# RWKV-7 and convolution decoder layer on one core: `a` rows transposed whole, first splits queued behind the squares, LayerNorm sums queued behind the gate products

## The chip, the core and the metric

The kernel runs on one core of one Trainium2 chip. The metric is the device time of one execution in microseconds (us). A core has five engines that matter here, each working through its own instructions in a fixed order: TensorE (PE in the profile; its weight loads are PEld), VectorE (DVE), ScalarE (ACT), GpSimd (POOL) and SyncE (SP, which here only issues DMAs). They meet through semaphores: an instruction that waits holds back all that stands behind it on its engine.

## The reference

One layer (depth 1, width 1024) is applied to a prompt of 2048 tokens and to 8 single sample tokens with stored states. Cut to what matters:

```python
h = rms_norm(x, norm_pre_g)
proj = h @ w_in                      # r | k | v | z_rwkv | two loras | glu (2 x 512) | z_conv | two gates
ps = token_shift(proj[..., :N_SHIFT])
# branch A, 16 heads of 64: S_t = S_{t-1} diag(w_t) + (S_{t-1} a_t) b_t^T + v_t k_t^T ;  y_t = S_t r_t
o_r = (group_norm(y_w) + bonus) * silu(z_r)
# branch B
u = (u1 + b1) * sigmoid(u2 + b2)
c = causal_depthwise_conv(u, conv_w, width 31) + conv_b
cn = (c - mean(c)) * rsqrt(var(c) + LN_EPS) * ln_c_g + ln_c_b
o_c = silu(cn) * silu(z_c)
merged = sigmoid(g_r) * (o_r @ w_branch_r) + sigmoid(g_c) * (o_c @ w_branch_c)
y = x + rms_norm(merged @ w_out, norm_post_g)
```

The new shift row, wkv state and convolution state come out too. All is fp32.

## The kernel before

**Blocks, units, fills.** The prompt is cut into four blocks of 512 tokens, and channels lie on the 128 partitions. In each block a loop over eight units (`j`, two heads of 64 each) runs `unit_in` (the projections of r, k, v, z for a later unit), `unit_a` (L505, all that needs no state) and `unit_b` (L660, the chunked state recurrence). Between units `fill` adds the work of the tables `FILL0` (block 0, L301), `FILL1` (blocks 1 and 2) and `FILL2` (block 3), one string a unit: `u` is one tile of GLU and convolution, `n` the LayerNorm mean, `z` and `Z` the two pairs of convolution gates, and a digit one pair of branch gates. Then come the branch products (`merge`) and the output product (`stage_out`). The sample tokens ride along: their projections are 8 columns of the products of block 0, and their recurrence is spread over blocks 1 and 2.

**What sets the order.** A scheduler orders every engine's instructions when the kernel is built: it takes what its own estimates call ready, by priority and program order, and the result is fixed. `tc.high_priority` and `later` move the priority, and `tc.issue_after(i)` puts instructions of the same engine behind `i` (`behind` (L193) is the same for several). Buffers count: a tile of tag `tmp` has four buffers, `x` two, `w` five, `wraw` three (L70). PSUM has eight banks: three `pg`, two `pa`, one each of `pb`, `pc`, `py`.

**A product** (`gemm`, L311) is three passes (high, low, high parts) over eight row tiles, in `pg` banks. In the trace it reads `pg<-ht,w`, 512 columns wide, or 264 wide in block 0. Weights come from HBM once (`wraw`), are split into a high half by ACT and a low half by DVE, and the split pair is written back (`kept`) and read from there in later blocks (`load_split`, L144). `gemm_first` (L433) is the first such product: four column blocks by two weight halves.

**The first stage** (`stage_first`, L391) loads eight tiles of x, squares them on ACT, adds the squares on DVE, sums over channels on PE (`py<-tmp,avg_c`), and scales and splits the tiles into `ht`.

**`unit_a`.** `ar` holds the `a` rows and the `r` rows of 8 chunks of 64 tokens, as [128, chunk, 2, 64], and `bk` the b and k rows. 32 matmuls of 64 x 64 stationary (`pa<-ar,bk`) form the scores, DVE masks them into `W` (`sc<-pa,maskw`), ACT copies diagonal blocks to `gd`, and DVE solves 32 x 32 triangular systems (`gp`, `zr`, `gd`). PE needs that solve's result at `pb<-gd,sc`. Beside it, `a` is turned to tokens by 16 matmuls of 64 x 64 against the identity (`pa<-ident,ar`; in fp32 each leaves two records) and copied by one ACT instruction to `aw`; 16 more (`pa<-xv,sc`) give the other half of `aw`; and 8 whole transposes (`pa<-ident,bk`, L649) turn `bk`. Each writes one of the two `pa` banks in turn, so the first four `bk` transposes need the bank that the first `aw` copy empties.

**Convolution branch.** The 30 further taps of a tile are DVE instructions (`et<-u,cw,et`) given out by `pull`. `conv_norm` (L764) adds the four tiles, sums over channels on PE (`pg<-tmp,avg_c`, queued behind the last product by `done`) and subtracts the mean. `conv_scale` (L775) squares, sums on PE in the same way, and applies scale, shift and swish. `conv_gate` (L794) makes a pair of z products.

Of the kernel before, what the change touches and what calls it, by code (L numbers as in the profile page):

```python
# [25 lines left out]
def rwkv7_conformer_step(  # L26
# [274 lines left out]
    FILL0 = ("u1", "u2", "u3", "u5", "6n", "7", "0", "4zZ")  # L301
# [131 lines left out]
    def gemm_first(ht, cols):  # L433
# [3 lines left out]
        for h in range(2):  # L437
            for c0 in cols:
                ws[c0, h] = new([128, 2, 4, 128], "w", F32R)
                load_split(ws[c0, h], win(c0)[h], ("in", c0 // 128, h))  # L440
# [64 lines left out]
    def unit_a(b, j, tw, ins):  # L505
# [34 lines left out]
        ar = new([128, NC, 2, C], "ar")  # L540
        stt(ar[:, :, 0, :], c3(kkn), -1.0, ep[:, :, 0:C], ALU.mult, ALU.mult)
# [6 lines left out]
        mul(ar[:, :, 1, :], c3(R), ep[:, :, 1:C + 1])  # L548
# [111 lines left out]
    def unit_b(b, j, parts):  # L660
# [19 lines left out]
        for hf in range(2):  # L680
# [613 lines left out]
```

## Time and profile before

| | us |
|---|---|
| three runs | 2786.7, 2793.33, 2791.29 |
| their median | 2791.29 |
| the profiled execution | 2793.45 |
| its span in the profile | 2791.7 |

The profile is of one execution. Busy times overlap between engines. A row of the order in time gives start, length, engine, line, what is written from what, shapes and a count; idle time before it stands in brackets with what ended it. Most helper operations carry the helper's line (L94 for ACT, L100 and L106 for DVE, L112 for matmuls), so groups are told apart by tile names.

### The profile page before, as it was taken

To read this page: it belongs to the slowest core of one execution; us is meant where nothing else is said; L and a number is where in the kernel's file an instruction comes from. 1 tells how busy PE (TensorE), PEld (TensorE's weight loads), DVE (VectorE), ACT (ScalarE), POOL (GpSimd) and SP (SyncE) were. 2 spreads that over 40 slices of the span, in tenths; PEclk is the share of its full clock that TensorE was granted. 3 is DMA by queue.
4 is the path that set the end of the run, shared out by engine and by line. 5 is a ranking of instruction groups with operands and counts; after the bars stand their busy time and mean duration, and the time that the engine had idled before them with its cause. 6 is when DMAs were issued, how large, how long until landed. Compare 5 with 4: busy or idle time off the path is not lost.

```text
span 2791.7 us, 55435 instructions
## 1 busy us (share of the span) xinstructions
PE 2675.3 (96%) x22800; PEld 2133.7 (76%) x22800; DVE 1768.0 (63%) x3856; ACT 1388.4 (50%) x3039; POOL 16.2 (1%) x61
## 2 busy tenths in 40 slices
PE   6999999989999998999999999999999999999998
PEld 6888888878877776776887777677798777777787
DVE  5688887667876547556576646676376755664412
ACT  5666656672344555656113565755411356566511
POOL 0000000000000000000000000000000000000000
PEclk9999999999999899999999999999999999999999
DMA  6555654547974253344666324244466522332484
GB/s 215 184 166 179 196 179 167 188 136 257 312 248 135 86 146 114 109 147 130 212 235 214 129 94 156 100 134 150 154 215 215 193 95 100 96 114 92 132 280 166
DMA packets 149648, 458.50 MB, mean 164 GB/s; under 512 B 18897, under 2 KB 24258, under 8 KB 149387
## 3 DMA queue, kind: packets, MB, share of 16 engines
q1 hardware_dynamic: 143441, 433.36, 47.0%
q10 hardware_dynamic: 5954, 21.60, 1.9%
q8 instruction: 179, 2.93, 0.4%
q14 instruction: 74, 0.61, 0.1%
HBM read 346.21 MB, written 109.16 MB: 163 GB/s over the span
## 4 chain that ended last, share of the span: by engine, by line
PE 58%; DVE 20%; ACT 14%; DMA 4%; issue 2%; SPq 0%; POOL 0%; DVEq 0%; ACTq 0%; POOLq 0%
PE pg L112 41%; PE pa L112 7%; DVE gd L100 4%; PE pc L112 4%; PE py L112 4%; DVE zr L610 4%; PE pb L112 2%; ACT sc L94 2%; DVE et L106 2%; DVE raw L106 2%; DMA wraw<-in_w_in_dram 2%; ACT tmp L94 2%; ACT xv L94 2%; ACT zbuf L94 1%; ACT keep L94 1%
## 5 line engine op out<-in xcount | busy, mean ns | idle before, releaser
L112 PE MATMUL pg<-ht,w 128*128 128x512 f32 (+1 forms) x7200 | 1539.8, 365 | 18.2 <-DVE sconv L109 6.5
L112 PEld LDWEIGHTS pg<-ht,w 128*128 128x128 f32 x7200 | 1172.8, 190 | 264.6 <-issue 63.9
L106 DVE SCALAR_TENSOR_TENSOR et<-u,cw,et 128x512 f32<-128x512 f32 x480 | 359.5, 749 | 8.2
L94 ACT ACTIVATE raw<-pg,omm 128x512 f32<-128x512 f32 (+1 forms) x155 | 93.8, 605 | 194.0 <-PE pg L112 189.8
L94 ACT ACTIVATE tmp<-tmp 128x512 f32<-128x512 f32 (+1 forms) x305 | 185.5, 630 | 5.0 <-DVE tmp L106 2.5
L112 PE MATMUL pg<-orr,w 128*128 128x512 f32 (+2 forms) x960 | 184.7, 349 | 0.0
L112 PEld LDWEIGHTS pg<-orr,w 128*128 128x128 f32 x960 | 154.7, 188 | 25.0 <-DVE x L100 0.2
L94 ACT ACTIVATE w<-wraw 128x512 fp32r<-128x512 f32 x162 | 101.4, 629 | 119.5 <-PE pg L112 70.5
L106 DVE SCALAR_TENSOR_TENSOR raw<-pg,prm,raw 128x511 f32<-128x511 f32 (+1 forms) x185 | 103.8, 573 | 84.6 <-ACT raw L94 83.8
L100 DVE TENSOR_TENSOR gd<-zr,gp 128x144 f32<-128x144 f32 (+10 forms) x512 | 139.9, 273 | 15.2
L610 DVE TENSOR_REDUCE zr<-gd 128x16 f32<-128x32 f32 (+15 forms) x512 | 136.9, 267 | 13.9 <-DVE gd L100 0.2
L100 DVE TENSOR_TENSOR w<-wraw,w 128x512 fp32r<-128x512 f32 x162 | 110.6, 685 | 46.3 <-ACT w L94 45.2
L94 ACT ACTIVATE gd<-sc 32x128 f32<-32x128 f32 x256 | 78.6, 307 | 114.5 <-DVE sc L100 108.4
L528 DVE TENSOR_TENSOR_SCAN tmp<-scanm,tmp 128x512 f32<-128x512 bf16 x32 | 39.1, 1223 | 137.3 <-ACT tmp L94 137.3
L94 ACT ACTIVATE xs<-pc,dk 128x64 f32<-128x64 f32 x224 | 70.2, 313 | 106.5 <-PE pc L112 106.0
L100 DVE TENSOR_TENSOR x<-x,pg 128x512 f32<-128x512 f32 (+1 forms) x80 | 46.1, 578 | 101.5 <-PE pg L112 36.4
L112 PE MATMUL pa<-ar,bk 64*64 64x128 f32 x2048 | 101.3, 279 | 5.2 <-DVE bk L100 3.1
L112 PEld LDWEIGHTS pa<-ar,bk 64*64 64x64 f32 x2048 | 77.5, 132 | 37.1 <-DVE bk L100 15.1
L94 ACT ACTIVATE x<-pg 128x512 f32<-128x512 f32 (+1 forms) x80 | 40.9, 511 | 123.7 <-PE pg L112 119.9
L100 DVE TENSOR_TENSOR sc<-pa,maskw 128x512 f32<-128x512 f32 x128 | 82.5, 684 | 30.7 <-PE pa L112 30.3
L94 ACT ACTIVATE sc<-pa 64x256 f32<-64x256 f32 (+1 forms) x192 | 73.1, 381 | 47.0 <-PE pb L112 43.7
L100 DVE TENSOR_TENSOR keep<-pa,raw 128x512 f32<-128x512 f32 x32 | 22.1, 692 | 109.5 <-PE pa L112 109.5
(359 smaller groups left out, 3694.8 us busy)
## 6 DMA issues: line engine op xcount, KB each, us to landing
w<-kept_in SPq DMA_DIRECT2D x366, 512.0 KB, 3.4
kept_in<-w SPq DMA_DIRECT2D x122, 512.0 KB, 3.8
wraw<-in_w_in_dram SPq DMA_DIRECT2D x122, 256.0 KB, 3.2
w<-kept_br SPq DMA_DIRECT2D x48, 512.0 KB, 4.1
w<-kept_out SPq DMA_DIRECT2D x40, 512.0 KB, 4.5
gate<-x ACTq DMA_DIRECT2D x24, 512.0 KB, 4.7
x<-gate SPq DMA_DIRECT2D x48, 256.0 KB, 4.1
w<-kept_bc SPq DMA_DIRECT2D x24, 512.0 KB, 3.2
```

Of the source, the lines that this page charges most:

```text
L94: return nc.scalar.activation(out=out, in_=in_, func=func, scale=scale, bias=bias, **kw)
L100: return nc.vector.tensor_tensor(out=out, in0=a, in1=b, op=op)
L106: return nc.vector.scalar_tensor_tensor(out=out, in0=a, scalar=s, in1=b, op0=op0, op1=op1)
L112: return nc.tensor.matmul(out=out, lhsT=lhsT, rhs=rhs, start=start, stop=stop, **kw)
L528: nc.vector.tensor_tensor_scan(out=sw, data0=scanm.rearrange("p c t -> p (c t)"), data1=sw, initial=0.0, op0=ALU.mult, op1=ALU.add)
L610: nc.vector.tensor_reduce(out=zl[:, 0:n, t:t + 2], in_=pr[:, 0:n, :, 0:w], axis=AX.X, op=ALU.add)
```

## The change

- `ar` becomes [128, 2, chunk, 64], so all `a` rows lie side by side. Four whole 128 x 128 transposes take the place of the 16 matmuls, and four ACT copies of 64 partitions take the place of one of 128. The score matmuls now read their 128 columns as two pieces of 64.
- `conv_norm` is called at the end of the first gate pair and `conv_scale` at the end of the second, each with its sum behind that pair's products. The gate products are kept in `x` tiles instead of `tmp`, and multiplied in at the end of `conv_scale`.
- `FILL0` puts `z` and `Z` at units 5 and 6, and gates 0 and 4 last.
- The splits of the first weights are queued behind the last square on ACT and behind the last addition on DVE.
- In block 0 the copies of the 8 sample columns out of PSUM go from DVE (`vcp`) to ACT (`cp`).
- The copy of the old convolution states from HBM to HBM is issued in block 1 instead of at the start.
- In the last block the output tile is multiplied by `norm_post_g` straight out of PSUM, scaled and added to x in one DVE instruction a half, and written as two DMAs.

```diff
-    FILL0 = ("u1", "u2", "u3", "u5", "6n", "7", "0", "4zZ")
+    FILL0 = ("u1", "u2", "u3", "u5", "6n", "z", "Z7", "04")
...
-                vcp(sraw[:, i, q, :], v.s[i])
+                cp(sraw[:, i, q, :], v.s[i])
...
-                tt(rb, rb, sq, ALU.add)
+                added = tt(rb, rb, sq, ALU.add)
+        first[:] = last.ins, added.ins
...
+        with behind(*first):
+            for h in range(2):
+                for c0 in cols:
+                    ws[c0, h] = new([128, 2, 4, 128], "w", F32R)
+                    load_split(ws[c0, h], win(c0)[h], ("in", c0 // 128, h))
...
-        ar = new([128, NC, 2, C], "ar")
+        ar = new([128, 2, NC, C], "ar")
...
-                           ar[es, c].rearrange("p a t -> p (a t)"))
+                           ar[es, :, c, :])
...
-        for c in range(NC):
-            for e, es in enumerate(ES):
-                mm(ps[es, c * C:c * C + C], ar[es, c, 0, :], ident[es, es])
-        cp(aw[:, :, 0, :], c3(ps))
+        for c2 in range(NC // 2):
+            nc.tensor.transpose(out=ps[:, c2 * 128:c2 * 128 + 128], in_=ar[:, 0, 2 * c2:2 * c2 + 2, :].rearrange("p c t -> p (c t)"),
+                                identity=ident)
+        awp = aw.rearrange("p (c i) a k -> p c i a k", i=2)
+        psv = ps.rearrange("p (c e k) -> p c e k", e=2, k=C)
+        for e in range(2):
+            for i in range(2):
+                cp(awp[ES[e], :, i, 0, :], psv[ES[i], :, e, :])
...
-        with tc.issue_after(done[0].ins):
+        with behind(done[0].ins):
...
             mul(cs[ct], cs[ct], s1)
+            mul(cs[ct], cs[ct], zgate[ct // 2][:, ct % 2])
...
-            s2 = new([128, BS], "tmp")
+        s2 = zgate[c0 // 2] = new([128, 2, BS], "x")
...
-        if c0 == 0:
-            conv_scale(b, cs)
-        for i, s2 in enumerate(s2s):
-            mul(cs[c0 + i], cs[c0 + i], s2)
+        (conv_scale if c0 else conv_norm)(cs)
...
-        with later(5000):
-            nc.scalar.dma_start(out=nconv_s[0, :, 0:NH - 1, :], in_=state_conv[0, :, 1:NH, :])
...
+        with behind(cp(un[0:NS], ps[0:NS]).ins):
+            nc.scalar.dma_start(out=nconv_s[0, :, 0:NH - 1, :], in_=state_conv[0, :, 1:NH, :])
...
-                    stt(osb[i][0:n, hs], pts[i][0:n] if h else osb[i][0:n, hs], rstd[0:n], gb[0:n, hs],
-                        ALU.mult, ALU.mult)
-                    tt(osb[i][0:n, hs], osb[i][0:n, hs], xrs[i][0:n, hs], ALU.add)
+                    stt(osb[i][0:n, hs], osb[i][0:n, hs], rstd[0:n], xrs[i][0:n, hs], ALU.mult, ALU.add)
+                    (nc.scalar, nc.sync)[h].dma_start(out=yout[:, hs], in_=osb[i][0:n, hs])
...
+                    if b == NB - 1:
+                        junk = new([128, 512], "tmp")
+                        act(junk[0:n], pts[i][0:n], AF.Square, accum_out=sq[i][0:n, h:h + 1])
+                        mul(half, pts[i][0:n], gb[0:n, h * 512:h * 512 + 512])
```

The scheduler moves instructions with it, at three places above all. **On PE, one unit of block 2, from its last score matmuls to the need of the solve** (names as above). Before:

```order
L112 MATMUL pa<-ar,bk 64x128 x16
L112 MATMUL pg<-ht,w 128x512 x3
L112 MATMUL pa<-ident,ar 64x64 x16
L112 MATMUL pa<-xv,sc 64x64 x16
L649 MATMUL pa<-ident,bk 128x128 x4
L112 MATMUL pg<-ht,w 128x512
L649 MATMUL pa<-ident,bk 128x128 x4
L112 MATMUL pg<-ht,w 128x512 x47
L112 MATMUL pb<-gd,sc 32x32 x16
```

The same unit now:

```order
L112 MATMUL pa<-ar,bk 64x128 x16
L112 MATMUL pg<-ht,w 128x512 x3
L640 MATMUL pa<-ident,ar 128x128 x4
L112 MATMUL pg<-ht,w 128x512
L112 MATMUL pa<-xv,sc 64x64 x16
L112 MATMUL pg<-ht,w 128x512 x4
L657 MATMUL pa<-ident,bk 128x128 x8
L112 MATMUL pg<-ht,w 128x512 x49
L112 MATMUL pb<-gd,sc 32x32 x16
```

The `ar` group stands apart from the `xv,sc` group, the `bk` group is in one piece behind four product matmuls, and between the `ar` group and the need of the solve stand 54 product matmuls where there were 48.

**On PE, block 1, around the second LayerNorm sum** (`pg<-tmp,avg_c`). Before:

```order
L112 MATMUL pa<-ident,ar 64x64 x16
L112 MATMUL pa<-xv,sc 64x64 x16
L649 MATMUL pa<-ident,bk 128x128 x4
L112 MATMUL pg<-ht,w 128x512
L649 MATMUL pa<-ident,bk 128x128 x4
L112 MATMUL pg<-ht,w 128x512 x2
L112 MATMUL pg<-tmp,avg_c 128x512
L112 MATMUL pg<-ht,w 128x512 x67
```

Now, one unit later in the block:

```order
L112 MATMUL pa<-tmp,ones_b 128x512
L112 MATMUL pg<-ht,w 128x512 x27
L112 MATMUL pa<-ar,bk 64x128 x32
L112 MATMUL pg<-tmp,avg_c 128x512
L640 MATMUL pa<-ident,ar 128x128 x4
L112 MATMUL pa<-xv,sc 64x64 x16
L112 MATMUL pg<-ht,w 128x512 x4
L657 MATMUL pa<-ident,bk 128x128 x8
```

The sum moved from behind the `bk` transposes to between the scores and the `ar` transposes, and no product stands between the two halves of the scores there.

**On ACT, the start** (`tmp<-x` and `tmp<-orr` are the squares of the eight x tiles, `w<-wraw` a weight split, `tmp<-py` the root of the sum). Before:

```order
L94 ACTIVATE tmp<-x 128x512 x4
L94 ACTIVATE tmp<-orr 128x512 x2
L94 ACTIVATE w<-wraw 128x512
L94 ACTIVATE tmp<-orr 128x512 x2
L94 ACTIVATE orr,ss<-orr 9x1024
L94 ACTIVATE w<-wraw 128x512
L94 ACTIVATE rstd<-ss,eps_rms 9x1
```

Now:

```order
L94 ACTIVATE tmp<-x 128x512 x4
L94 ACTIVATE tmp<-orr 128x512 x4
L94 ACTIVATE xs<-state 128x64
L94 ACTIVATE zr<-grp 128x8x4
L94 ACTIVATE orr,ss<-orr 9x1024
L94 ACTIVATE tmp<-py,eps_rms 128x512
L94 ACTIVATE rstd<-ss,eps_rms 9x1
```

No split stands among the squares any more: the first comes behind the first `ht` tile, and the first low half on DVE behind the seventh `ht` tile. On SP, three `wraw` loads are followed by three `kept` writes before the fourth load; before, only one write stood between the third and the fourth load.

## Rows read from the trace of the kernel before

**Rows 1.** The page: busy time of each engine (part 1), the shares of the chain that ended last by engine (part 4), and of the table of PE's waits (engine, tile, line <- what it waited for: us in total, times, longest) five rows.
```profile
PE 2675.3 (96%) x22800; PEld 2133.7 (76%) x22800; DVE 1768.0 (63%) x3856; ACT 1388.4 (50%) x3039; POOL 16.2 (1%) x61
...
PE 58%; DVE 20%; ACT 14%; DMA 4%; issue 2%; SPq 0%; POOL 0%; DVEq 0%; ACTq 0%; POOLq 0%
...
PE pb L112 <- DVE gd L612: 20.2, 22, 2.2
PE py L112 <- DVE tmp L100: 15.0, 1, 15.0
PE pg L112 <- DVE tmp L100: 10.9, 2, 6.8
PE pg L112 <- DVE sconv L109: 6.5, 4, 1.9
PE pa L649 <- ACT aw L94: 3.4, 6, 0.9
```

**Rows 2.** PE in order of time in one unit of block 2, and the stretch around it in the table by stretches (us, busy and instructions of PE, PEld, DVE, ACT, POOL, then granted clock, DMA share, GB/s).
```profile
1587.15 0.97 PE L112 MATMUL pa<-ident,ar 64*64 64x64 f32 x26
...
1588.09 0.98 PE L112 MATMUL pa<-xv,sc 64*64 64x64 f32 x27
1589.06 0.66 PE L649 MATMUL pa<-ident,bk 128*128 128x128 f32 x4
1589.47 0.48 PE L112 MATMUL pg<-ht,w 128*128 128x512 f32 x1
1589.78 0.64 PE L649 MATMUL pa<-ident,bk 128*128 128x128 f32 x4
1590.17 2.10 PE L112 MATMUL pg<-ht,w 128*128 128x512 f32 x8
...
1586.00:1594.00 8.00, 8.00 (x103) 6.46 (x96) 6.29 (x16) 5.15 (x9) 0.00 (x0) 1.00 0.21 68
```

**Rows 3.** ACT copies: four of 64 partitions in a row in the order of time, and the `aw` copy in the view of that tile (duration ns min/median/max).
```profile
57.32 1.55 ACT L94 ACTIVATE xv<-pb 64x256 f32<-64x256 f32 x4
...
L94 ACT ACTIVATE aw<-pa x64: 577/597/604, 85.4 to 2602.2; 128x512 f32<-128x512 f32 x64
```

**Rows 4.** PE groups by shape (busy us, mean ns of one | idle before).
```profile
L112 PE MATMUL pa<-ar,bk 64*64 64x128 f32 x2048 | 101.3, 279 | 5.2 <-DVE bk L100 3.1 <-DVE sc L100 1.9
...
L112 PE MATMUL pa<-xv,sc 64*64 64x64 f32 x1024 | 38.6, 224 | 0.6 <-ACT xv L94 0.5
```

**Rows 5.** Block 1, PE in order of time around the second LayerNorm sum, and the two stretches there.
```profile
1105.22 2.08 PE L112 MATMUL pg<-tmp,avg_c 128*128 128x512 f32 x2 [6.83 <-DVE tmp L100]
...
1098.00:1106.00 8.00, 1.17 (x3) 0.50 (x2) 8.00 (x20) 4.05 (x7) 0.00 (x0) 0.81 0.19 67
1106.00:1114.00 8.00, 8.00 (x27) 5.90 (x26) 8.00 (x21) 5.34 (x8) 0.00 (x0) 0.77 0.36 130
```

**Rows 6.** The end of block 0: PE in order of time, and three stretches.
```profile
614.34 4.72 PE L112 MATMUL pg<-ht,w 128*128 128x264 f32 x24 [4.03 <-DVE tmp L100]
...
620.04 0.49 PE L112 MATMUL pg<-ht,w 128*128 128x512 f32 x1 [0.99 <-ACT ht L94]
...
606.00:614.00 8.00, 4.31 (x36) 4.09 (x34) 4.50 (x8) 8.00 (x16) 0.00 (x0) 1.00 0.41 131
614.00:622.00 8.00, 6.09 (x28) 5.17 (x28) 7.67 (x15) 6.42 (x14) 0.00 (x0) 0.76 0.56 160
622.00:630.00 8.00, 7.89 (x29) 6.11 (x29) 7.99 (x15) 3.13 (x6) 0.00 (x0) 0.81 0.18 62
```

**Rows 7.** The start in order of time: the state copy on ACT's DMA queue, then ACT, DVE, PE and SP.
```profile
1.46 0.78 ACTq L967 DMA_DIRECT2D out_dram<-in_state_conv_dram  x1
...
11.26 1.32 ACT L94 ACTIVATE tmp<-orr 128x512 f32<-128x512 f32 x2
...
15.92 0.63 ACT L94 ACTIVATE w<-wraw 128x512 fp32r<-128x512 f32 x1 [3.35 <-DMA wraw<-in_w_in_dram]
16.46 1.14 ACT L94 ACTIVATE tmp<-orr 128x512 f32<-128x512 f32 x2
16.59 0.69 DVE L100 TENSOR_TENSOR w<-wraw,w 128x512 fp32r<-128x512 f32 x1 [3.78 <-ACT w L94]
...
17.73 0.38 SPq L151 DMA_DIRECT2D wraw<-in_w_in_dram  x1
...
19.62 2.05 PE L112 MATMUL py<-tmp,avg_c 128*128 128x512 f32 x2 [14.98 <-DVE tmp L100]
...
26.37 1.03 PE L112 MATMUL pg<-ht,w 128*128 128x264 f32 x3 [2.58 <-ACT ht L94]
...
52.48 3.58 PE L112 MATMUL pg<-ht,w 128*128 128x264 f32 x28
```

**Rows 8.** The end in order of time, behind the last matmul.
```profile
2783.89 0.60 ACT L94 ACTIVATE orr<-pg 128x512 f32<-128x512 f32 x1 [4.13 <-PE pg L112]
...
2785.37 0.75 DVE L106 SCALAR_TENSOR_TENSOR orr<-orr,rstd 128x512 f32<-128x512 f32 x1 [0.60 <-ACT rstd L94]
2786.04 0.75 DVE L106 SCALAR_TENSOR_TENSOR orr<-pg,rstd,orr 128x512 f32<-128x512 f32 x1
2786.70 1.28 DVE L100 TENSOR_TENSOR orr<-orr,x 128x512 f32<-128x512 f32 x2
2788.02 0.34 ACTq L1097 DMA_DIRECT2D out_dram<-orr  x1
```

More of the change, by code (lines that the diff above doesn't have):

```diff
@@ L389, in stage_a @@
         return ht
+    first = []
     def stage_first():
@@ L436, in gemm_first @@
         views, ws = [], {}
[L437 to L440, printed above, removed]
+        with behind(*first):
[3 more added lines that the diff above has]
+                    load_split(ws[c0, h], win(c0)[h], ("in", c0 // 128, h))
         for i, _ in enumerate(cols):
@@ L539, in unit_a @@
         stt(kkn, K, pv("kk", j), kkn, ALU.mult, ALU.mult)
-        ar = new([128, NC, 2, C], "ar")
-        stt(ar[:, :, 0, :], c3(kkn), -1.0, ep[:, :, 0:C], ALU.mult, ALU.mult)
+        ar = new([128, 2, NC, C], "ar")
+        stt(ar[:, 0], c3(kkn), -1.0, ep[:, :, 0:C], ALU.mult, ALU.mult)
         mul(kkn, kkn, ic)
@@ L547, in unit_a @@
         mul(bk[:, :, 1, :], c3(K), c3(em))
-        mul(ar[:, :, 1, :], c3(R), ep[:, :, 1:C + 1])
+        mul(ar[:, 1], c3(R), ep[:, :, 1:C + 1])
         stt(R, R, pv("rk", j), K, ALU.mult, ALU.mult)
@@ L688, in unit_b @@
             tt(MY[:, cs, 0, :], psv[:, :, 0, :], id2.unsqueeze(1).to_broadcast([128, 4, C]), ALU.add)
-            tt(MY[:, cs, 1, :], psv[:, :, 1, :], ar[:, cs, 1, :], ALU.add)
+            tt(MY[:, cs, 1, :], psv[:, :, 1, :], ar[:, 1, cs, :], ALU.add)
         xs = new([128, NC, C], "xs")
@@ L756, in glu @@
             if b == 0:
-                vcp(sconv[:, ct, :], va.s[0])
-                vcp(sconv[:, CT + ct, :], vb.s[0])
+                cp(sconv[:, ct, :], va.s[0])
+                cp(sconv[:, CT + ct, :], vb.s[0])
         vcp(hist[:, ct, :], ub[:, BS:BS + NTAP - 1])
@@ L762, in glu, with conv_norm @@
         return acc
-    def conv_norm(b, cs):
+    def conv_norm(cs):
         sm = new([128, BS], "tmp")
@@ L773, in conv_norm, with conv_scale @@
             tt(cs[ct], cs[ct], ps, ALU.subtract)
-    def conv_scale(b, cs):
+    def conv_scale(cs):
         sm = new([128, BS], "tmp")
@@ L782, in conv_scale @@
             tt(sm, sm, sq, ALU.add)
-        with tc.issue_after(done[0].ins):
+        with behind(done[0].ins):
             ps = stat(pgt, avg_c, sm)
@@ L792, in conv_scale @@
             mul(cs[ct], cs[ct], s1)
+            mul(cs[ct], cs[ct], zgate[ct // 2][:, ct % 2])
+    zgate = [None, None]
     def conv_gate(b, ht, cs, c0):
         vs = gemm([hspec(b, ht, N_SHIFT + 2 * DC + (c0 + i) * 128) for i in range(2)])
-        s2s = []
+        s2 = zgate[c0 // 2] = new([128, 2, BS], "x")
         for i, z in enumerate(vs):
-            ct = c0 + i
-            s2 = new([128, BS], "tmp")
-            s2s.append(s2)
             with tc.high_priority(HPZ):
-                sigmoid_v(s2, z)
+                sigmoid_v(s2[:, i], z)
                 for ps, sl in z.parts:
-                    mul(s2[:, sl], s2[:, sl], ps)
+                    mul(s2[:, i, sl], s2[:, i, sl], ps)
                 if b == 0:
-                    vcp(sconv[:, 2 * CT + ct, :], z.s[0])
-        if c0 == 0:
-            conv_scale(b, cs)
-        for i, s2 in enumerate(s2s):
-            mul(cs[c0 + i], cs[c0 + i], s2)
+                    cp(sconv[:, 2 * CT + c0 + i, :], z.s[0])
+        (conv_scale if c0 else conv_norm)(cs)
     def conv_split(b, cs):
@@ L1022, in gate @@
                 if b == 0:
-                    vcp(gate_s[:, i0 + i, :], v.s[0])
+                    cp(gate_s[:, i0 + i, :], v.s[0])
         act(s, s, AF.Ln, bias=1.0)
@@ L1096, in finish @@
                 tt(osb[i][0:n], osb[i][0:n], xrs[i][0:n], ALU.add)
-            nc.scalar.dma_start(out=yout, in_=osb[i][0:n])
+                nc.scalar.dma_start(out=yout, in_=osb[i][0:n])
         for h in range(2):
@@ L1117, in sums @@
                     half = osb[i][0:n, h * 512:h * 512 + 512]
-                    act(half, pts[i][0:n], AF.Square, accum_out=sq[i][0:n, h:h + 1])
-                    if not (b == NB - 1 and h == 1):
+                    if b == NB - 1:
+                        junk = new([128, 512], "tmp")
+                        act(junk[0:n], pts[i][0:n], AF.Square, accum_out=sq[i][0:n, h:h + 1])
+                        mul(half, pts[i][0:n], gb[0:n, h * 512:h * 512 + 512])
+                    else:
+                        act(half, pts[i][0:n], AF.Square, accum_out=sq[i][0:n, h:h + 1])
                         cp(half, pts[i][0:n])
```

2 lines of the change are left out of this document (removed).

## The prediction

> **What bounds the kernel now.** I read the page's busy times first, then the table of PE's waits, then the order in time at the places that the change touches. PE is busy 96% of the span, DVE 63%, ACT 50% [rows 1]: PE sets the time, and the other engines cost only where PE waits for them. So the change is worth what it takes out of PE's work and out of PE's waits. The waits have names [rows 1]: 20.2 us in 22 places for the triangular solve on DVE, 15.0 us once for the first sum, 10.9 us in two places for DVE's `tmp` (6.8 us of it is the second LayerNorm sum of block 1 [rows 5]), 6.5 us in four for the copies `sconv`, 3.4 us for `aw`. Work that is added to ACT or DVE is free until one of these waits grows.
>
> All sums are made against the profiled execution, 2793.45 us, which stands 2.2 us above the median 2791.29.
>
> **The transposes, on PE.** In the unit shown the 16 small matmuls run from 1587.15 to the main run of the next group at 1588.09: 0.94 us. Four whole transposes take 0.41 us (1589.06 to the product at 1589.47) or 0.39 us (1589.78 to 1590.17) [rows 2]. Saved: 0.54 us a unit, 17 us for 32. Against that, PE changes between kinds of work once more per unit (the `ar` group now stands alone, the `bk` group is whole). The single product between the two `bk` groups takes 0.31 us (1589.47 to 1589.78), against 0.24 us in a row of eight ((2.10 - 0.39) / 7) [rows 2]; I take 0.12 us for a change of kind, a little over that 0.07 us, 4 us in all. Net -13 us, between -17 us and -5 us (a change as dear as 0.38 us).
>
> **The four copies, on ACT.** Four copies of 64 partitions took 1.55 us in a row, the one they replace 0.60 us [rows 3]: +0.95 us a unit, 30 us more on ACT, which goes from 50% to 51%. Who waits for them: the first `bk` transpose, for its bank. What covers them in the new order: one product, the 16 small matmuls (0.97 us, 1588.09 to 1589.06) and four products, 0.24 + 0.97 + 0.96 = 2.2 us [rows 2], where the copies take 1.55 us behind the `gd` copies in ACT's queue. So they are just covered. If the cover fails everywhere it costs 0.95 us in each unit, 30 us. But in the 22 units in which PE waits for the solve anyway, a wait here only shortens that one; ten units are left, and I take 0.3 us in each: +3 us, between 0 and +30 us. The Trainium skill (ScalarE: Activation LUTs, What ACT_TABLE_LOAD costs) says that ScalarE instructions back to back overlap by about 93 ns; by that, four copies would take about 1.25 us and ACT would carry some 20 us more instead of 30. The row of 1.55 us shows no such overlap for these, and the sum goes by the row.
>
> **The wait for the solve.** Between the `ar` group and the solve's need stand 54 products where there were 48 (the order on PE, block 2): 6 x 0.24 = 1.4 us more work in the window, less 0.54 us for the transposes. DVE's chain is as long as before, so a wait of 20.2 / 22 = 0.9 us should shrink. Other windows of other units gain less or lose, and what moves in here is missing elsewhere. I take -5 us, between -12 us and +3 us.
>
> **The split read.** The score matmuls read two pieces of 64 columns. Nothing in the trace shows such a read of 128 columns. It can't be faster than one piece, so 0 is one bound. The other: each record as two of 64 columns, 2 x 38.6 / 1024 = 75 ns against 101.3 / 2048 = 49 ns now [rows 4], +26 ns x 2048 = +53 us. I take 0: the columns are as many, and the stationary side, which is loaded for each, is unchanged.
>
> **LayerNorm sums and gate products.** In block 1 the second sum stood two products behind the transposes, and PE idled 6.83 us before it, in a stretch at a granted clock of 0.81 and followed by one at 0.77 [rows 5]. Its squares can only begin behind the gate products, since `tmp` has four buffers and the gates held two; DVE was busy all of 1098 to 1106. Now the gates lie in `x`, and the sum stands a unit later. But it stands between the scores and the `ar` transposes with no product in front, so DVE's additions (two of 0.69 us, behind two of the four masks) are waited for openly. I take -5 us for the wait that goes (0 to -8 us with the clock) and +3 us for new waits at the eight sums (0 to +20 us, if three are as long as this one).
>
> **The end of block 0.** `4zZ` put the whole scale chain at the block's end: ACT is busy 8.00 of 8 us and PE 4.31 us from 606 to 614, PE then idles 4.03 and 0.99 us in front of products, and the granted clock averages 0.76 and 0.81 in the two stretches of 8 us that follow [rows 6], 1.9 + 1.5 us of full speed. Together 8.4 us. With `04` there only two gates, without that chain, stand at the end. I take -7 us, between -9 us and 0 (gate 7 now follows `Z` and needs an `x` tile that `conv_scale` frees).
>
> **Small copies to ACT.** DVE was late four times with `sconv`, 6.5 us [rows 1]. 94 small copies go to ACT, which has room. -4 us, between -6.5 us and +3 us (ACT's queue is in order, and the copies stand among evictions).
>
> **The start.** The split in front of the last two squares held ACT until 15.92 us while the tiles before had been squared by 12.58 us; the last square ended at 17.60 us, the sum ran at 19.62 us, and products began at 26.37 us [rows 7]. Without the split, and without the state copy that was issued at 1.46 us on DMA engines that the x tiles need, squares can end 3.7 us earlier or more. But the low halves of the weights now stand behind seven `ht` tiles on DVE: the first was done at 17.3 us [rows 7] and will be some 14 us later. SP is in order: the fourth weight load, at 17.73 us before [rows 7], stands behind three writes that wait for three low halves, so it moves to about 33 us, and the fourth column block starts at about 37 us. First products begin some 6 us earlier, then PE waits for weights, and the four first blocks end where they did, at 52.48 us [rows 7]. I take 0, between -4 us and +4 us.
>
> **The end.** Behind the last matmul two scalings (0.67 us apart) and a pair of additions 1.28 us long led from 2785.37 to the DMA at 2788.02 [rows 8]: 2.65 us. Now two instructions of 0.75 us lead to two DMAs: 1.42 us, 1.2 us less, and each DMA carries half. -2 us, between -1 us and -3 us. The moved copy of states costs block 1 nothing visible.
>
> **The sum.** -13 + 3 - 5 + 0 - 5 + 3 - 7 - 4 + 0 - 2 = -30 us: 2763 us in a profiled execution like this one, 2761 us as a median.
>
> **The rivals.**
> - *PE's saved time is waited away.* The solve and the copies are the bound in each unit: PE saves 0.44 us and stands that much longer at `pb<-gd,sc` in 22 units (+10 us), and the copies cost the other ten units 0.95 us (+10 us). For it speak the 22 waits; against it the extra products in the window. 2781 us.
> - *The sums take over.* Three of the eight LayerNorm sums wait some 6 us each at their new places: +15 us over the forecast, 2776 us. For it: DVE lagged so in block 1 [rows 5]. Against it: seven of the eight did not wait in the profile's two `tmp` waits.
> - *More than forecast.* The solve wait goes entirely (-15 us more) and the start gives 4 us: 2742 us.
> - *Slower: the split read restarts each score matmul.* At its full price of +53 us the time is 2814 us. The change is a loss from 30 us on, that is 15 ns for each of the 2048 records. For it speaks only that no such read is in the trace.
> - *Slower: the clock.* The Trainium skill (TensorE: Matmul & The Clock Gate, Part 4: PE-mode transpose) says that a transpose doesn't count as PE activity for the clock. As a mechanism here: four more transposes in each unit pull the granted clock down once a unit, as from 622 to 630 us, at 0.81, 1.5 us [rows 6]: 32 x 1.5 = 49 us, 2810 us. Against it: the stretch with eight transposes shows a granted clock of 1.00 [rows 2], and low stretches follow idle PE [rows 5, 6].
>
> **How the numbers follow.** Chances: the forecast (2746 to 2777 us) 0.60, time waited away 0.17, the sums 0.08, more than forecast 0.08, split read 0.04, clock 0.03. The predicted time is the forecast's, 2761 us. The range leaves out the two slower cases and the outer parts of the others: 2738 to 2788 us. A measurement of this kernel can tell about 0.2% from no change, 5.6 us: below 2785.7 us is faster, above 2796.9 us slower. Faster: 0.60 + 0.08 + 0.07 and most of 0.17, together 0.85; slower 0.07; the same 0.08.
>
> **What would show it.** Right, if four `ar` transposes take about 0.4 us, if `bk` waits little for `aw`, if the wait for the solve falls from 20.2 us, if no sum is waited for over 2 us, if PE runs through 606 to 622 us, and if the score group keeps its 101 us. Wrong, if that group grows by over 30 us, if `pb<-gd,sc` waits longer, if PE stands at a LayerNorm sum or at gate 7 in block 0, or if products of the first four column blocks end later than 55 us.

## The result, and the profile after

| | us |
|---|---|
| kernel before, median of 5 runs (2786.7 to 2795.25) | 2793.33 |
| changed kernel, median of 5 runs (2765.75 to 2770.51) | 2768.27 |
| ratio, with its 95% interval | 0.9917 [0.9903, 0.9931] |
| span in the profile, before and after | 2791.7, 2766.5 |

The changed kernel is faster by 25 us. The forecast was 30 us, with 2761 us in a range from 2738 to 2788. First the page and PE's waits, as in [rows 1] (engine, tile, line <- what it waited for: us in total, times, longest).

```profile
PE 2669.0 (96%) x21904; PEld 2117.5 (77%) x21904; DVE 1755.1 (63%) x3761; ACT 1415.8 (51%) x3226; POOL 16.1 (1%) x61
...
PE pa L657 <- ACT aw L94: 13.5, 28, 1.5
...
PE py L112 <- DVE tmp L100: 9.5, 1, 9.5
...
PE pg L112 <- ACT tmp L94: 6.0, 4, 4.7
...
PE pb L112 <- DVE gd L616: 4.3, 9, 1.1
...
PE pg L112 <- ACT sconv L94: 3.6, 3, 2.3
...
PE pg L112 <- DVE tmp L100: 1.0, 1, 1.0
```

Against [rows 1]: the wait for the solve fell from 20.2 to 4.3 us, that of `pg` for DVE's `tmp` from 10.9 us (6.8 us at a LayerNorm sum and 4.0 us at a product at the end of block 0 [rows 5, 6]) to 1.0 us, that for `sconv` from 6.5 to 3.6 us, the one for the first sum (`py`) from 15.0 to 9.5 us, and the wait of the `bk` transposes for `aw` rose from 3.4 to 13.5 us. What PE is busy with fell by 6.3 us, its time without work (span less busy) from 116.4 to 97.5 us, by 18.9 us.

A unit of block 2, PE and then ACT in order of time, and the stretch, as in [rows 2]:

```profile
1578.59 0.66 PE L640 MATMUL pa<-ident,ar 128*128 128x128 f32 x4
1579.00 0.48 PE L112 MATMUL pg<-ht,w 128*128 128x512 f32 x1
...
1582.03 1.28 PE L657 MATMUL pa<-ident,bk 128*128 128x128 f32 x8 [0.34 <-ACT aw L94]
...
1594.82 0.69 PE L112 MATMUL pb<-gd,sc 32*32 32x32 f32 x32
...
1578.00:1586.00 8.00, 7.66 (x65) 5.71 (x65) 5.76 (x15) 5.94 (x12) 0.00 (x0) 1.00 0.26 85
```
```profile
1579.28 0.38 ACT L94 ACTIVATE aw<-pa 64x256 f32<-64x256 f32 x1
1579.56 0.58 ACT L94 ACTIVATE x<-pg 128x512 f32<-128x512 f32 x1
1580.17 0.62 ACT L94 ACTIVATE gd<-sc 32x128 f32<-32x128 f32 x2
1580.81 1.78 ACT L94 ACTIVATE aw<-pa 64x256 f32<-64x256 f32 x4
```

The four transposes take 0.41 us (1578.59 to 1579.00), as forecast. The solve is no longer waited for here. But the four copies don't stand in a row: behind the first, ACT evicts a product (`x<-pg`) and makes two `gd` copies (the last row holds the other three copies and the one of the second half of `aw`), and PE waits 0.34 us in front of `bk`.

Block 0, where the LayerNorm work now lies: PE in order of time, then four stretches.

```profile
526.16 1.47 PE L112 MATMUL pg<-ht,w 128*128 128x264 f32 x5 [2.33 <-ACT sconv L94]
...
564.38 0.69 PE L112 MATMUL pa<-ar,bk 64*64 64x128 f32 x4 [3.60 <-DVE bk L100]
```
```profile
614.00:622.00 8.00, 8.00 (x101) 6.33 (x95) 0.00 (x0) 4.68 (x14) 0.00 (x0) 1.00 0.01 2
...
530.00:538.00 8.00, 7.98 (x81) 5.90 (x79) 0.69 (x1) 5.66 (x15) 0.00 (x0) 0.60 0.20 69
562.00:570.00 8.00, 4.01 (x34) 2.37 (x34) 7.46 (x13) 4.22 (x9) 0.00 (x0) 0.61 0.67 230
570.00:578.00 8.00, 7.53 (x89) 6.16 (x89) 4.88 (x8) 6.23 (x15) 0.00 (x0) 0.75 0.01 2
```

The stop at the end of block 0 [rows 6] is gone, and PE runs through at full clock. In its place PE stands in the two gate units, 2.33 us up to 526 us for a `sconv` copy on ACT and 3.60 us up to 564 us for DVE, which is busy 7.46 of 8 us, and the granted clock falls to 0.60 and 0.61 there.

The second sum of block 1 [rows 5]:

```profile
1150.67 0.44 PE L112 MATMUL pa<-ar,bk 64*64 64x128 f32 x4 [0.83 <-DVE bk L100]
1151.99 1.09 PE L112 MATMUL pa<-ar,bk 64*64 64x128 f32 x28 [0.89 <-DVE bk L100]
1154.46 2.57 PE L112 MATMUL pa<-ar,bk 64*64 64x128 f32 x32 [1.38 <-DVE sc L100]
1156.96 2.07 PE L112 MATMUL pg<-tmp,avg_c 128*128 128x512 f32 x2
```

The sum itself is not waited for; the scores in front of it are, for 3.1 us, where the old place cost 6.83 us.

A wait that nobody forecast, in block 0, on SP's queue, ACT and PE:

```profile
301.94 0.44 SPq L517 DMA_DIRECT2D wraw<-in_w_lora_dram  x1
```
```profile
310.39 0.42 ACT L94 ACTIVATE lora_w<-wraw 128x256 fp32r<-128x256 f32 x1 [4.63 <-DMA wraw<-in_w_lora_dram]
...
311.22 1.47 PE L112 MATMUL pg<-ht,w 128*128 128x264 f32 x5 [4.66 <-ACT tmp L94]
```

The same load in the DMA issues of the kernel before (what, queue, times, KB each, median us from issue to landing; this is the only one of the 32 whose landing that trace tells):

```profile
wraw<-in_w_lora_dram SPq DMA_DIRECT2D x32, 192.0 KB, 8.8
```

A load of 192 KB was issued at 301.94 us and used at 310.39; four other such loads, whose landing the trace tells, took 3.0 to 3.6 us. The load was no faster before: issued at 303.19 us, it took 8.8 us, but ACT came to its copy only at 315.43 us and did not wait. What is new is ACT's order. ACT is in order, so an eviction behind the copy, and with it PE, stood for 4.66 us (the longest of the four waits for ACT's `tmp` above).

Start and end, against [rows 7] and [rows 8]:

```profile
13.78 2.05 PE L112 MATMUL py<-tmp,avg_c 128*128 128x512 f32 x2 [9.47 <-DVE tmp L100]
...
31.78 2.45 SPq L151 DMA_DIRECT2D wraw<-in_w_in_dram  x3
...
54.19 6.15 PE L112 MATMUL pg<-ht,w 128*128 128x264 f32 x48
```
```profile
2762.20 1.42 DVE L106 SCALAR_TENSOR_TENSOR orr<-orr,rstd,x 128x512 f32<-128x512 f32 x2
2762.99 0.34 ACTq L1097 DMA_DIRECT2D out_dram<-orr  x1
```

The first sum ran 5.8 us earlier, and the fourth weight load was issued at 31.78 us (17.73 before); the first four column blocks gave way to the next products at 54.19 us (52.48 before). The last two scalings began at 2762.20 us, and the first DMA left 0.79 us later.

**Where the time lies.** The next table is worked out from PE's order of time: the first `pg<-orr,w` (the branch products) of each block and the last matmul part the run into stages. It is used for all experiments below. Each row is one execution: e4 and e10 (the first splits alone, the split read alone), which took as long as the kernel before, and the two rows of the changed kernel show that a block can differ by some 4 us without a cause in the edit.

| us | block 0 | block 1 | block 2 | block 3 | output |
|---|---|---|---|---|---|
| before | 661.8 | 695.3 | 673.0 | 640.2 | 113.2 |
| changed | 669.1 | 678.4 | 663.5 | 636.2 | 113.1 |
| e1, transposes alone | 662.8 | 689.9 | 674.8 | 644.4 | 113.4 |
| e3, norm and gates alone | 665.5 | 693.4 | 668.9 | 638.1 | 111.9 |
| e4, first splits alone | 661.1 | 697.0 | 674.6 | 639.1 | 112.4 |
| e10, split read alone | 662.1 | 695.8 | 674.7 | 638.9 | 112.0 |
| e9, both | 665.1 | 687.0 | 663.7 | 636.0 | 113.3 |
| e11, changed again | 669.9 | 682.3 | 664.0 | 635.8 | 113.1 |
| e7, rows turned early | 657.1 | 676.7 | 660.0 | 635.0 | 113.0 |

Block 0 lost 7.3 us; block 1 gained 16.9, block 2 9.5 and block 3 4.0 us.

### The profile page after: what moved, and what is told of

Same layout as the page of the kernel before. It is cut to its first block, busy times and chain, and to the rows that moved or that the text cites. A ratio compares the mean times of both kernels' runs of the same rounds, so it can differ in the third digit from the quotient of the medians.

```text
span 2766.5 us, 53792 instructions
## 1 busy us (share of the span) xinstructions
PE 2669.0 (96%) x21904; PEld 2117.5 (77%) x21904; DVE 1755.1 (63%) x3761; ACT 1415.8 (51%) x3226; POOL 16.1 (1%) x61
## 4 chain that ended last, share of the span: by engine, by line
PE 65%; DVE 15%; ACT 14%; DMA 3%; issue 2%; POOL 0%; SPq 0%; DVEq 0%; ACTq 0%; POOLq 0%
PE pg L112 45%; PE pa L112 8%; PE pc L112 4%; PE py L112 4%; DVE gd L100 3%; DVE zr L614 3%; ACT sc L94 2%; PE pb L112 2%; DVE raw L106 2%; ACT zbuf L94 2%; ACT tmp L94 1%; ACT aw L94 1%; ACT gd L94 1%; ACT xv L94 1%; ACT keep L94 1%
## 5 line engine op out<-in xcount | busy, mean ns | idle before, releaser
L94 ACT ACTIVATE tmp<-tmp 128x512 f32<-128x512 f32 (+1 forms) x273 | 165.8, 629 | 4.9 <-DVE tmp L106 3.5
L94 ACT ACTIVATE x<-pg 128x512 f32<-128x512 f32 (+1 forms) x100 | 50.7, 508 | 138.6 <-PE pg L112 138.1
L100 DVE TENSOR_TENSOR x<-x,pg 128x512 f32<-128x512 f32 (+1 forms) x100 | 57.3, 577 | 93.3 <-PE pg L112 39.9
L94 ACT ACTIVATE x<-x 128x1024 f32<-128x1024 f32 (+1 forms) x96 | 87.7, 913 | 1.5
```

Source lines behind the costliest of these rows:

```text
L94: return nc.scalar.activation(out=out, in_=in_, func=func, scale=scale, bias=bias, **kw)
L100: return nc.vector.tensor_tensor(out=out, in0=a, in1=b, op=op)
```

## The experiments

Three chips served: e1 to e4 ran on the first, e5 to e8 on the second, e9 to e12 on the third. The kernel before took 2798.5, 2786.8 and 2798.3 us (medians) on them, and each ratio is against the kernel before on the same chip. The changed kernel stands at 0.9917 in the result and at 0.9907 on the third chip (e11); among the runs on the second there is none of it. There e8 stands nearest to it, at 0.9937, so what e5, e6 and e7 show against the changed kernel is given against both marks.

| run | median us | ratio [95% interval] |
|---|---|---|
| e1 transposes alone | 2792.10 | 0.9980 [0.9971, 0.9989] |
| e2 state copy alone | 2794.12 | 0.9986 [0.9976, 0.9995] |
| e3 norm and gates alone | 2791.85 | 0.9977 [0.9967, 0.9986] |
| e4 first splits alone | 2795.93 | 0.9995 [0.9985, 1.0005] |
| e5 changed, without transposes | 2780.06 | 0.9974 [0.9965, 0.9983] |
| e6 changed, without norm and gates | 2784.95 | 0.9994 [0.9985, 1.0003] |
| e7 changed, rows turned early | 2749.28 | 0.9873 [0.9858, 0.9888] |
| e8 changed, rms on ACT's queue | 2770.55 | 0.9937 [0.9924, 0.9949] |
| e9 transposes and norm together | 2774.55 | 0.9907 [0.9893, 0.9920] |
| e10 split read alone | 2795.25 | 0.9990 [0.9978, 1.0001] |
| e11 changed kernel again | 2773.43 | 0.9907 [0.9893, 0.9920] |
| e12 small copies alone | 2800.76 | 1.0005 [0.9995, 1.0016] |

**e1, the transposes alone.** Into the kernel before:

```diff
-        ar = new([128, NC, 2, C], "ar")
+        ar = new([128, 2, NC, C], "ar")
...
-                mm(ps[es, c * C:c * C + C], ar[es, c, 0, :], ident[es, es])
-        cp(aw[:, :, 0, :], c3(ps))
+            nc.tensor.transpose(out=ps[:, c2 * 128:c2 * 128 + 128], in_=ar[:, 0, 2 * c2:2 * c2 + 2, :].rearrange("p c t -> p (c t)"),
+                                identity=ident)
...
+                cp(awp[ES[e], :, i, 0, :], psv[ES[i], :, e, :])
...
```

> The kernel before with the new a-row layout, the four whole transposes and the four copies, and nothing else. Theory read from the two profiles: the group of the a rows falls from 28 to 15 us (-13), the wait for the solve from 20 to about 4 us (-16), while PE waits some 10 us more for the copies, the score groups grow 5 us and the further changes of kind cost 5 us or so: together about -9 us, between -5 and -13. Rival, the sum of the prediction: -13 + 3 - 5 + 0 = -15 us. Second rival: the saved time is waited away at the solve, 0 to -3 us, with the wait for the solve still near 20 us.

Measured: -6.4 us between the medians. PE's waits in e1, its order of time at the second sum of block 2 and near that of block 3, and the stretches there:

```profile
PE pg L112 <- DVE tmp L100: 14.4, 5, 6.2
PE pa L653 <- ACT aw L94: 12.5, 29, 1.2
...
PE pb L112 <- DVE gd L612: 5.3, 11, 0.9
```
```profile
1776.67 2.08 PE L112 MATMUL pg<-tmp,avg_c 128*128 128x512 f32 x2 [6.15 <-DVE tmp L100]
...
2429.97 0.44 PE L112 MATMUL pa<-ar,bk 64*64 64x128 f32 x4 [1.74 <-DVE bk L100]
...
1770.00:1778.00 8.00, 1.85 (x5) 0.58 (x3) 7.49 (x23) 3.93 (x7) 0.15 (x1) 0.71 0.24 83
1778.00:1786.00 8.00, 8.00 (x79) 4.88 (x80) 1.43 (x4) 6.95 (x17) 0.19 (x1) 0.50 0.01 2
...
2434.00:2442.00 8.00, 6.91 (x70) 5.39 (x71) 5.40 (x9) 5.48 (x15) 0.00 (x0) 0.50 0.01 2
```

The waits moved as the theory has it, and the size fits the lower end of its range. But the waits at the LayerNorm sums grew from 6.8 us (one sum) to 9.6 us (2.5, 6.2 and 0.9 us at three; the rest of the 14.4 us is at products at the end of block 0): PE, faster now, reaches a sum in block 2 that DVE has not finished (7.49 of 8 us busy), stands 6.15 us, and runs the next 8 us at half clock. In block 3 it is not the sum: PE stands at scores and `ar` transposes shortly before the second sum, four times for DVE and 5.2 us in all (2.0 us at this place before), and runs the 8 us from 2434 us at half clock. In this execution blocks 2 and 3 took 1.8 and 4.2 us more than before, 0.2 and 5.3 us more than in e4 on the same chip: what the transposes save is lost there.

**e3, norm and gates alone.** Into the kernel before:

```diff
-    FILL0 = ("u1", "u2", "u3", "u5", "6n", "7", "0", "4zZ")
+    FILL0 = ("u1", "u2", "u3", "u5", "6n", "z", "Z7", "04")
...
-        s2s = []
+        s2 = zgate[c0 // 2] = new([128, 2, BS], "x")
...
-        if c0 == 0:
-            conv_scale(b, cs)
-        for i, s2 in enumerate(s2s):
-            mul(cs[c0 + i], cs[c0 + i], s2)
+        (conv_scale if c0 else conv_norm)(cs)
...
```

> The kernel before with only the LayerNorm sums behind the gate products, the gates in x tiles and the new table of block 0. Theory read from the two profiles: the gain (end of block 0: 5.6 us idle and 3.4 us of clock; second sum of block 1: 6.8 us idle and 3.4 us of clock) is given back at new waits in the gate units of block 0 (7.5 us idle and two stretches of 10 us at half clock) and of block 1 (3.1 us idle and 7 us at half clock): together between 0 and +8 us, about +4. Rival, the sum of the prediction: -5 + 3 - 7 = -9 us.

Measured: -6.6 us. The theory (a loss) fell; the prediction's -9 us is nearer. The theory was right on block 0, which is 3.7 us longer (PE stands 4.66 us from 557 us on and 2.27 us up to 526 us); the gain lies in blocks 1 to 3.

**e9, both together.**

> The kernel before with two parts of the change, the transposes (as e1) and the sums with the gates and the new table (as e3), and nothing else. Theory: the two parts need each other, since the sums' new places take away the waits at which e1 lost its gain: together more than the sum of both alone, -18 to -24 us, 0.9914 to 0.9936. Rival: they add, -5.6 - 6.4 = -12 us, 0.9957. Second rival: what e5 and e6 showed comes from the other parts together, and the two alone give less than their sum, 0.997 or more.

Measured: 0.9907, the ratio of the whole change (e11), and -24 us between the medians, where -6.4 and -6.6 would add to -13. In e9 the wait for the solve, the same sum and its stretch read:

```profile
PE pb L112 <- DVE gd L612: 3.0, 10, 0.4
...
1765.91 1.02 PE L112 MATMUL pg<-tmp,avg_c 128*128 128x512 f32 x2
...
1763.00:1771.00 8.00, 8.00 (x35) 6.09 (x33) 7.57 (x23) 1.86 (x3) 0.00 (x0) 1.00 0.46 147
```

The sum is not waited for, and the clock stays at 1.00. By stages, e1 and e3 added would change blocks 0 to 3 by +4.7, -7.3, -2.3 and +2.1 us; e9 has +3.3, -8.3, -9.3 and -4.2. What the two parts give to each other lies in blocks 2 and 3, where e1 lost its time.

**e5 and e6, the changed kernel with one of these parts taken back** (e5: the edit of e1 undone; e6: that of e3 undone).

> The changed kernel with the old a-row layout, the 16 small matmuls and the one copy back, all else as changed. The changed kernel stands at 0.9917 of the kernel before. Theory: the transposes give more here than alone, because the LayerNorm sums at which e1 lost its gain (6.15 us idle at 1770 us, and 13.65 and 10.24 us at half clock) stand elsewhere now: without them the time is 10 us or more longer than the changed kernel's, 0.9953 or above, and the wait for the solve is back at 15 to 20 us. Rival: the parts simply add, 5.6 us as in e1 alone, 0.9937. Second rival: the transposes are worth nothing here, since PE waits 13.5 us for their copies, 0.9917.

> The changed kernel with the old LayerNorm sums, gates in tmp and the old table of block 0, all else as changed. Theory: the saved PE time lets PE reach the old sums before DVE does, as in e1: waits of 3 to 7 us at the sums of blocks 1 and 2 and half clock behind them, so 10 to 14 us longer than the changed kernel, 0.9953 to 0.9967 of the kernel before. Rival: the parts add, 6.4 us as in e3 alone, 0.9940.

PE's wait for the solve in e5, and the second sum of block 2 in e6:

```profile
PE pb L112 <- DVE gd L616: 21.3, 24, 3.7
...
1772.68 2.08 PE L112 MATMUL pg<-tmp,avg_c 128*128 128x512 f32 x2 [6.16 <-DVE tmp L100]
```

Measured: 0.9974 and 0.9994. In e5 the wait for the solve is back at 21.3 us; in e6 PE stands 6.2 us at the same sum as in e1. The direction of both theories holds, and e6 went beyond the range of its ratio. How much each part is worth in company depends on the mark: the transposes 18 us and the sums 23 us against 25 us for the whole change, but 10 and 14 us by e8 on the same chip. From e1, e3 and e9, on two chips on which the kernel before took the same time, each part is worth 17 us on top of the other. By each of the three accounts both are worth more in company than the 6.5 us that each gives alone.

**e2, the state copy alone.** Into the kernel before:

```diff
-        with later(5000):
-            nc.scalar.dma_start(out=nconv_s[0, :, 0:NH - 1, :], in_=state_conv[0, :, 1:NH, :])
...
-        vcp(un[0:NS], ps[0:NS])
+        with behind(cp(un[0:NS], ps[0:NS]).ins):
+            nc.scalar.dma_start(out=nconv_s[0, :, 0:NH - 1, :], in_=state_conv[0, :, 1:NH, :])
```

> The kernel before with only the copy of the old convolution states moved from the start into block 1, and the copy of the new state row in front of it on ACT. Theory: this is what gathers the 16 scattered pairs of small sample products (read pb<-u,orr) in block 1 into two groups, since the order on PE shows 2 groups here and 16 before. They cost 0.33 us of idle PE each in front and drew the granted clock to 0.5 for 17 us behind them: -9 us for the changes of kind and -6 for the clock, together -15 us (between -8 and -18), at about 949 to 970 us. Rival, as in the prediction: the move costs and gives nothing, 0 us (between -3 and +3).

Measured: -4.4 us. PE in block 1 of the kernel before (one of 16 such places, and the stretch), then of e2:

```profile
953.31 0.59 PE L112 MATMUL pb<-u,orr 64*128 64x8 f32 x2
953.83 0.79 PE L112 MATMUL pg<-ht,w 128*128 128x512 f32 x1
...
952.00:960.00 8.00, 8.00 (x21) 4.78 (x21) 2.39 (x9) 1.51 (x5) 0.00 (x0) 0.55 0.18 52
```
```profile
953.24 1.96 PE L112 MATMUL pb<-u,orr 64*128 64x8 f32 x16
```

The pairs are gathered as the theory says, but no idle PE stood in front of them (PE is busy 8.00 of 8 us), and block 1 is 6.8 us shorter where the theory had 15. The granted clock from 950 to 974 us is 0.86 in e2 and was 0.64, which is 5 of these 6.8 us. Block 0 is 6.5 us longer (PE reaches its first solve 2.4 us later, and 3.9 us more go between the fourth and the fifth), which the theory did not have; why is not shown.

**e4, the first splits alone.** The splits of `gemm_first` stand in `with behind(*first)`, and nothing else changes.

> The kernel before with only the first weight splits queued behind the last square and the last addition. Theory: the first sum comes some 5 us earlier on PE, but the first low halves stand behind the ht tiles on DVE and PE waits for them, so that the end of the first four column blocks does not move: 0 us (between -2 and +3). Rival: the earlier sum is kept, -4 to -6 us. Second rival: the late splits also push the fourth weight load on SP, and the end of the first blocks comes later, +3 to +6 us.

Measured: 0.9995, no difference clear of noise, as the theory and the prediction have it.

**e10, the split read alone.**

```diff
...
-                           ar[es, c].rearrange("p a t -> p (a t)"))
+                           ar[es, :, c, :])
...
-                mm(ps[es, c * C:c * C + C], ar[es, c, 0, :], ident[es, es])
+                mm(ps[es, c * C:c * C + C], ar[es, 0, c, :], ident[es, es])
...
```

> The kernel before with the new layout of the a and r rows alone: the 16 small matmuls and the one copy stay, and only the 2048 score records read their 128 columns as two pieces of 64. Theory read from the two profiles (score group 101.3 us before, 103.8 us in the changed kernel): +2 to +5 us, 1.0007 to 1.0018, the score group at 103 to 106 us. Rival, the prediction's value: 0 us. Second rival, the prediction's upper bound: each record restarts, +53 us, 1.019, the score group near 154 us.

```profile
L112 PE MATMUL pa<-ar,bk 64*64 64x128 f32 x2048 | 101.3, 279 | 5.2 <-DVE bk L100 3.1
```

The score group takes the same 101.3 us as in [rows 4]. The split read is free, so the 2.5 us by which the group grew in the changed kernel have another cause, probably where it stands in PE's order. The theory was wrong, the prediction's 0 right.

**e12, the small copies alone.**

```diff
...
-                vcp(sconv[:, ct, :], va.s[0])
+                cp(sconv[:, ct, :], va.s[0])
...
```

> The kernel before with only the 94 small copies of sample columns moved from DVE to ACT. The prediction: -4 us, 0.9986, between -6.5 and +3, with the wait for sconv falling from 6.5 us. Rival, from the changed kernel's profile, where PE still waits 3.6 us for sconv and 1.3 us for the gates' copies on ACT: -2 to 0 us, 0.9993 to 1.0, since ACT's queue is late where DVE's was.

Measured: 1.0005, no gain. ACT and PE in e12:

```profile
316.04 0.42 ACT L94 ACTIVATE lora_w<-wraw 128x256 fp32r<-128x256 f32 x1 [4.87 <-DMA wraw<-in_w_lora_dram]
...
317.56 1.06 PE L112 MATMUL pb<-zbuf,gp 32*32 32x32 f32 x32 [8.09 <-ACT gp L94]
```

PE still waits 6.1 us for `sconv`, and 8.09 us once for a copy behind the late lora load in ACT's queue.

**e8, the small write on another queue.** In the changed kernel:

```diff
-        nc.sync.dma_start(out=rms_d[b].rearrange("t p -> p t"), in_=rs)
+        nc.scalar.dma_start(out=rms_d[b].rearrange("t p -> p t"), in_=rs)
```

> The changed kernel with the small write of the row scales (rms, 2 KB) issued on ACT's DMA queue instead of SP's; nothing is left out. In the changed kernel's trace the load of the lora weights stands behind that write in SP's queue, takes 8.4 us to land, ACT stands 4.63 us for it, and PE 4.66 us at 306.6 us with 6.83 us at half clock behind. Theory: the small packets held up the queue, the load lands in some 3 us, and the time falls by 5 to 8 us, 0.9894 to 0.990. Rival: the packets hold up the DMA engines whichever queue they come from, 0.9917. Second rival: the wait goes, but block 0 waits elsewhere as long, 0.9910 to 0.9917.

Measured: 0.9937, no gain over the changed kernel's 0.9917 and 0.9907, and the wait is still there. SP, ACT and one stretch in e8:

```profile
302.97 0.43 SPq L517 DMA_DIRECT2D wraw<-in_w_lora_dram  x1
...
311.77 0.42 ACT L94 ACTIVATE lora_w<-wraw 128x256 fp32r<-128x256 f32 x1 [5.00 <-DMA wraw<-in_w_lora_dram]
...
304.00:308.00 4.00, 3.17 (x24) 2.96 (x24) 3.66 (x13) 0.96 (x3) 0.00 (x0) 1.00 0.15 8
```

The load takes 8.8 us, where it took 8.4 us in the changed kernel, while the DMA engines move 8 GB/s. Which queue the small write is in made no difference. That the write is the cause is not shown: it stands ahead of the load, but so do writes of split weights (`kept`) in SP's queue, and neither was left out.

**e7, the rows turned early.** In the changed kernel the block from `aw = new(...)` to the four copies moves up behind the copies of `xv`, with the `pb` bank:

```diff
...
         aw = new([128, NC, 2, C], "aw")
-        ps = pa()
+        ps = pb()
...
```

> The changed kernel with the four transposes and their four copies in front of the score matmuls, in the pb bank, instead of behind the masks in a pa bank; nothing is left out. Theory: the copies are the wait (13.5 us in 28 places at the bk transposes), and there is enough other work for the solve: the wait goes, the time falls by 8 us, between 4 and 13: 0.989 of the kernel before. Rival: DVE's solve is the bound of each unit and takes the time back, the wait for the solve grows from 4.3 to 12 us or more, and the time stays at 0.9917. Second rival: the bk transposes wait as long for the one copy that is left between the banks, and nothing changes.

```profile
PE pb L112 <- DVE gd L627: 10.2, 18, 1.4
...
PE pa L658 <- ACT aw L94: 1.4, 4, 0.5
```

Measured: 0.9873, faster than both kernels: 10 and 12 us against the changed kernel's two ratios, 21 us against e8 on the same chip, where the theory had 8 us, at most 13. Theory and rival both hold in part: the wait for `aw` fell from 13.5 to 1.4 us, and the solve took 5.9 of these 12.1 us back (4.3 to 10.2). In blocks 1 to 3 this is 1.7, 3.5 and 1.2 us against the changed kernel's profile. The other 12.0 us lie in block 0. There ACT's wait for the lora load is gone, since its copy stands later in ACT's order (at 311.77 us, with no wait); how much more of the 12 us is the copies' and how much the order's stays open.

**e11, the changed kernel again.**

> The changed kernel as it is, on the chip of the other three runs, as the mark for e5 to e9: 0.9917 of the kernel before, between 0.990 and 0.9935. If it stands at 0.989 or below, the gain of e7 over it would be within the uncertainty; at 0.994 or above, e5 and e6 would tell less of what each part gives.

Measured: 0.9907. The intervals of e11 and e7 don't overlap, nor do those of e8 and e7.

## Why the prediction was right, and where it was not

The time was right, and so was what bounds the kernel: PE's work and PE's waits, place by place. What was not right is **the sum**: it prices each part at its own place and has no term for what one part does to another. Alone the transposes and the sums give some 6.5 us each, together 24 us (e9). PE that is faster by 0.4 us a unit runs into DVE near the LayerNorm sums of blocks 2 and 3 (e1), which the prediction, reading a wait only in block 1 [rows 5], did not see; with the sums moved neither wait is there, and the granted clock from 1350 to 2650 us is 1.00 (e9).

That the total came so near is in part luck. The terms for the transposes (-15 us) and for the sums and the end of block 0 (-9 us) give the -24 us that e9 measured, but by other amounts within. Shared evenly over the blocks that they touch, the terms of the forecast make -14 us in block 0, -14 us in blocks 1 to 3 and -2 us behind the last matmul; the profiles have +7.3, -30.4 and -2.0 us. An error of 21 us one way and one of 16 us the other way nearly cancel.

- *Transposes, -13 us.* The duration was right (0.41 us). On top of the moved sums (e3 to e9) blocks 0 to 3 fell by 0.4, 6.4, 5.2 and 2.1 us (14.1 us; the output stage rose by 1.4; between the medians it is 17 us), against the forecast -15 us for transposes, copies and solve.
- *Copies, +3, and solve, -5 us.* Mis-sized both: +10.1 and -15.9 us. The prediction let the four copies follow in a row, with 2.2 us of cover. In the unit shown the cover was there (2.7 us, from 1579.0 us until PE stood at 1581.7), but ACT puts an eviction and `gd` copies among the four. PE waits for them in 28 places, where the prediction priced ten units. That wait stands ahead of the solve's and shortens it, as the prediction says. The two terms together are -5.8 us where -2 was forecast; e7 shows that the copies' part was only half a loss.
- *Split read, 0 us.* Right (e10). The rival at 2814 us falls.
- *Sums, -5 and +3 us.* In block 1 near: 6.83 us gave way to 3.1 us, and e3's block 1 is 1.9 us shorter. In block 0 the new waits were taken too small, and in blocks 2 and 3 the gain was missed.
- *End of block 0, -7 us.* The place was right and the sign of the block wrong: the idle PE and the low clock are gone there, but the same DVE and ACT work stops PE in the two gate units, and block 0 is 3.7 us longer in e3.
- *Small copies, -4 us.* Wrong for the copies alone: e12 gives no gain. ACT's queue is in order too, and had a late load in it. In company with the other parts they were not tried.
- *Start, 0, and end, -2 us.* Right: e4 shows no difference for the splits alone, and from the last matmul's start to the end of the span it is 6.2 us (2766.5 - 2760.3) where it was 8.2 (2791.7 - 2783.5).
- *The moved copy of states, 0 us.* Wrong: it gathers 16 scattered pairs of small products in block 1, and alone gives 4.4 us (e2).
- *The waits that take the place of those removed.* The rival in which saved time is waited away holds for e1 and not for the change. The clock rival falls: the stretch with twelve transposes has a granted clock of 1.00, and so has the changed kernel over 1350 to 2650 us, with four more transposes in every unit. The Trainium skill's sentence that transposes do not count as activity in the same way (TensorE: Matmul & The Clock Gate, Part 4: PE-mode transpose) is neither borne out nor refuted by this, since products of 512 columns stand around the transposes.

The parts that remain, taken against e9, cancel: block 0 is 4.0 us longer in the changed kernel (the lora load's 4.66 us lie there) and block 1 4.7 to 8.6 us shorter, most likely by the gathered products. The clock's part of this differs from execution to execution: from 950 to 974 us the granted clock is 0.64 in the kernel before and 0.68 in e9, but 0.93 and 0.79 in the two profiles of the changed kernel, which against e9 is 6 and 2.6 us of full speed. That is nearly the 3.9 us by which these two differ in block 1 (678.4 and 682.3).

## What to carry to other kernels

Where a change speeds up the bounding engine and moves the work it would next wait for, price the two together: here each alone gave a quarter of what both gave. After a saving on PE, look in every block for the next wait whose releaser is already busy almost all of the stretch (DVE 7.46 and 7.49 of 8 us here), not only for the waits that the trace shows now. A group of copies that is priced as a row must be found as a row in the copying engine's order.

## What was not expected of the hardware

A 192 KB load of lora weights took 8.4 to 8.8 us at one place (kernel before, changed kernel, e8), where four others of the changed kernel took 3.0 to 3.6 us, and the DMA engines moved 8 GB/s from 304 to 308 us of e8. Ahead of it in time stand a write of 512 pieces of 4 bytes, in either of two queues, and writes of split weights; which of them holds it up was not tried. The granted clock fell to 0.55 from 952 to 960 us of the kernel before while PE was busy all 8.00 us, in a stretch that alternates products of 8 columns with products of 512; every other low stretch shown here followed idle PE.
